# A hybrid SSD and forgetting-attention step on one core: values and dt columns by tokens, gate tiles spread over the stages

## The chip, the cores and the metric

The kernel runs on one core of one Trainium2 chip. The time is device microseconds of one execution; before the change the median of three runs is 2090.52 us (2086.51 to 2091.22). Lines named L242 and the like are lines of the kernel before.

## The reference, cut to what matters

One layer for 1024 new tokens of one stream and 16 tokens each of eight running streams, 1152 tokens in all, with a model width of 1024. One input projection yields the columns of two branches. The result, the new keys and values and the new states are returned.

```python
h = jnp.einsum('bld,de->ble', x, w_in)
z, xbc, dt_raw, q, k, v, f_raw, g_path, mg_m, mg_a = split_projection(h)
xbc, new_conv = causal_conv(xbc, conv_state, conv_w, conv_b)
dt = jax.nn.softplus(dt_raw + dt_bias)            # 32 heads
y, new_ssm = ssd_scan(xs, dt, A, Bm, Cm, s0, chunk)  # 8 groups
y_m = group_rms((y + d_skip * xs) * silu(z)) * mnorm_w
logf = jax.nn.log_sigmoid(f_raw + b_f)            # 16 heads
o = fox_prompt(q, k, v, logf)                     # and fox_sample, with caches
y_a = o * jax.nn.silu(g_path)
u = sigmoid(mg_m + b) * (y_m @ w_br_m) + sigmoid(mg_a + b) * (y_a @ w_br_a)
x_new = layer_norm(DN_ALPHA * x + u @ w_out, ln_g, ln_b)
```

## The kernel before, in words

Every f32 operand of a large product is split into a high and a low part of a reduced type, and a product becomes three: high by high, low by high, high by low. The input x stands in SBUF for the whole first half, as eight blocks of 128 rows (model width) by three chunks of 384 tokens, high and low. One **column tile** (`dense`, L257) is 128 output columns: for each of three chunks a PSUM bank gets 8 × 3 products (`passes`, L242 to L244, 128 by 128 stationary weights, 384 tokens moving) and is then taken out by a function that depends on the columns. So a column tile is 72 products, and its output has channels on partitions and tokens along the row. `fetch` and `split` (L202, L212) bring the next weight tile and split it, ScalarE the high part, another engine the low part.

The stages, in order:

1. **Head** (L311 to L339): x is loaded and split, and a column tile of only 48 columns (dt and forget columns) is computed, with channels on partitions; `tables` then transposes it to tokens (L357) and makes the decay tables from it.
2. **SSD stage**: eight groups of six column tiles (`group_dense`); beside the tiles of a group runs the scan of the group before (`group`). Behind the last group stand six of the 16 **gate tiles** (`gate_dense`, L717), whose output goes to DRAM.
3. **Attention stage** (FOX): eight pairs of heads. `pair_dense` computes four column tiles of a pair: values, gate path, queries, keys. The values must have tokens on partitions later, so 2 ticks after each of three banks three transposes (a **turn**, L745) and a copy bring them to `vt`. Beside the four tiles of a pair runs the attention of the pair before (`pair`), by a plan written out by hand: a list of ticks with what is issued at each. Beside the last pair run four gate tiles.
4. **Remaining gate tiles**: six, during which the SSD result is scaled. `ssr` loads sums of squares, takes root and reciprocal, writes `rs_d`; `load_rows` loads four blocks of rows (`yr`) and the scale (`rsb`), multiplies (L1151) and splits (L1154 ScalarE, L1155 VectorE) into `ya0`.
5. **Merge**: `quarter` and `whole` multiply the branch results by the branch weights into `acc`, apply the gates, then the output product (L1263 to L1265) and the layer norm.

What runs beside the tiles is a generator; `Flow` counts a tick for every two steps of eight in a bank, and lets the generator issue more when its ticks are used up. Inside `tc.manual_schedule()` instructions stay in the order written on each engine; outside, a scheduler orders them by priority. A pool of SBUF that reuses the room of a closed pool waits for that pool as a whole.

Of the kernel before, what the change touches and what calls it, by code (L numbers as in the profile page):

```python
# [11 lines left out]
F32 = mybir.dt.float32  # L12
# [22 lines left out]
GATES_SSD = 6  # L35
# [9 lines left out]
def in_tiles():  # L45
# [102 lines left out]
def trunk_step(ctx: ExitStack, tc: tile.TileContext, I, O):  # L148
# [35 lines left out]
    gate_d = dr.tile([16, P, T], F32, name="gate_d")  # L184

# [10 lines left out]
    todo = [(I["wdtf"], None, KT * 48)]  # L196
    todo += [(I["wt"][i], scale, 1024) for i, (_, scale) in enumerate(in_tiles())]
# [59 lines left out]
    def dense(rhs, evac, m=P):  # L257

        hi, lo = next_w()
        for c in range(NCH):  # L260
            d = bank(f"d{count[0]}_{c}")[:m, :CW]
            passes(d, KT, lambda k: (hi[:, k * m:(k + 1) * m], lo[:, k * m:(k + 1) * m]),
                   lambda k: (rhs[c][0][:, k, :], rhs[c][1][:, k, :]), lambda: evac(c, d))
# [23 lines left out]
    spa = ssd_stack.enter_context(tc.tile_pool(name="spa", bufs=1))  # L287


    pro_stack = ExitStack()  # L290
    pp = pro_stack.enter_context(tc.tile_pool(name="pp", bufs=1))
    dbf = pp.tile([48, 1], F32, name="dbf")
    sgn = pp.tile([48, 1], F32, name="sgn")
# [6 lines left out]
    dtf = pp.tile([48, T], F32, name="dtf")  # L300
# [4 lines left out]
    fones = pp.tile([P, P], F32, name="fones")  # L305

# [4 lines left out]
    fetch()  # L311
    split(more=False)
    ve.memset(sgn[0:32, :], 1.0)
    ve.memset(sgn[32:48, :], -1.0)
    for c in range(NCH):
        for h in range(4):
            k = slice(2 * h, 2 * h + 2)
            xr = pp.tile([P, 2, CW], F32, tag="xr", name=f"xr{c}_{h}", bufs=4)
            sy.dma_start(xr[:], I["xT"][c][:, k, :])
            ac.copy(X[c][0][:, k, :], xr[:])  # L320
            ve.tensor_tensor(X[c][1][:, k, :], xr[:], X[c][0][:, k, :].bitcast(F32), ALU.subtract)  # L321
        if c == 0:
            sy.dma_start(dbf[:], I["dtfb"])
    fetch()
    sy.dma_start(ident[:], I["ident"])
    sy.dma_start(cst[:], I["const"])
    sy.dma_start(cpro[:], I["const2"])
    sy.dma_start(alog[:], I["a_log"].to_broadcast([P, 32]))
    sy.dma_start(dsk[:], I["d_skip"].to_broadcast([P, 32]))
# [1048 lines left out]
```

## Time and profile before

| | |
|---|---|
| median of 3 runs | 2090.52 us |
| the profiled execution, its own time | 2090.63 us |
| its span | 2088.8 us |
| TensorE with work in flight | 2060.0 us, 14495 products |
| VectorE busy | 1331.9 us |
| ScalarE busy | 820.7 us |
| GpSimd busy | 615.8 us |
| granted TensorE clock, mean | 0.999 |
| mean DMA rate | 136 GB/s |

Times are in us from the span's start, unless marked ns. PE is TensorE, DVE VectorE, ACT ScalarE, POOL GpSimd, SP SyncE, whose queue issues most transfers. A row of a timeline has start, duration, engine, line, operation, output and inputs, shapes and a count; what follows in brackets is the time that the engine stood idle before it and what ended that. The durations of products overlap, since the array is pipelined; what a product costs is the distance from one start to the next.

### The profile page before, as it was taken

What the parts mean: (1) busy time and instruction counts of PE and PEld (TensorE: products, weight loads), DVE (VectorE), ACT (ScalarE), POOL (GpSimd) and SP (SyncE); (2) the same over time, 40 slices, a digit from 0 to 9 for tenths busy, and PEclk for the clock granted to TensorE, in tenths of its full rate; (3) what the DMA queues carried; (4) which work ended last, traced back from release to release, by engine and by line L of the source; (5) the groups of instructions that cost most, each with busy time, mean ns of one, the idle gap of its engine ahead of it and who ended that gap; (6) DMA issues with size and microseconds to landing.
All of it is one profiled execution on the core that took longest, in us unless ns stands there. A gap on an engine that the chain in (4) does not pass through costs nothing.

```text
span 2088.8 us, 36542 instructions
## 1 busy us (share of the span) xinstructions
PE 2060.0 (99%) x14495; PEld 1897.9 (91%) x14495; DVE 1331.9 (64%) x2252; ACT 820.7 (39%) x1662; POOL 615.8 (29%) x789
## 2 busy tenths in 40 slices
PE   8999999999999999999999999999999999999998
PEld 7998989898989898999889888889889999999987
DVE  7577777777777776514776866876765343182355
ACT  3344444444444343324455454454453442122210
POOL 1146465645555554510011011011111021113400
PEclk9999999999999999999999999999999999999999
DMA  5213242423232424443555555555564653154222
GB/s 169 81 55 106 88 121 81 133 76 127 76 117 77 126 76 133 133 153 100 199 177 190 189 193 170 190 193 176 182 204 148 219 195 108 41 188 154 86 100 91
DMA packets 110748, 283.07 MB, mean 136 GB/s; under 512 B 18041, under 2 KB 67185, under 8 KB 100337
## 3 DMA queue, kind: packets, MB, share of 16 engines
q1 hardware_dynamic: 98032, 199.46, 30.3%
q10 hardware_dynamic: 12544, 81.27, 11.2%
q8 instruction: 114, 1.87, 0.4%
q14 instruction: 58, 0.47, 0.1%
HBM read 228.89 MB, written 51.79 MB: 134 GB/s over the span
## 4 chain that ended last, share of the span: by engine, by line
PE 69%; DVE 18%; DMA 5%; ACT 4%; issue 2%; POOL 2%; SPq 0%; ACTq 0%; DVEq 0%; POOLq 0%
PE d L242 16%; PE d L244 15%; PE d L243 15%; PE o L903 3%; DVE m L605 3%; PE s L828 3%; DMA ce<-ac_d 2%; PE so L978 2%; PE out L1263 2%; PE out L1265 2%; PE out L1264 2%; PE dq L242 2%; PE dq L244 2%; PE dq L243 2%; DVE m L609 2%
## 5 line engine op out<-in xcount | busy, mean ns | idle before, releaser
L242 PE MATMUL d<-xh,wh 128*128 128x384 f32 (+1 forms) x2328 | 820.0, 352 | 16.9 <-ACT xh L320 6.2
L244 PE MATMUL d<-xh,wl 128*128 128x384 f32 (+1 forms) x2328 | 781.8, 336 | 0.1
L243 PE MATMUL d<-xl,wh 128*128 128x384 f32 (+1 forms) x2328 | 780.6, 335 | 0.8 <-DVE xl L321 0.7
L242 PEld LDWEIGHTS d<-xh,wh 128*128 128x128 f32 (+1 forms) x2328 | 436.1, 187 | 57.6 <-issue 18.1
L243 PEld LDWEIGHTS d<-xl,wh 128*128 128x128 f32 (+1 forms) x2328 | 436.7, 188 | 4.1 <-DVE xl L321 2.0
L244 PEld LDWEIGHTS d<-xh,wl 128*128 128x128 f32 (+1 forms) x2328 | 435.7, 187 | 1.7 <-DVE wl L225 0.4
L222 POOL TENSOR_TENSOR wl<-wr,wh 128x1024 fp32r<-128x1024 f32 (+1 forms) x58 | 137.6, 2372 | 319.5 <-ACT wh L221 304.6
L605 DVE TENSOR_SCALAR m<-ce,nacum 128x128 f32<-128x128 f32 x288 | 119.2, 455 | 49.5 <-DMA ce<-ac_d 49.4
L221 ACT CAST wh<-wr 128x1024 fp32r<-128x1024 f32 (+1 forms) x73 | 75.8, 1038 | 182.1 <-PE d L243 157.1
L833 ACT ACTIVATE st<-s,ckt 128x256 f32<-128x256 f32 (+1 forms) x320 | 115.0, 465 | 44.6 <-PE s L828 42.5
L225 DVE SCALAR_TENSOR_TENSOR wl<-wr,wh 128x1024 fp32r<-128x1024 f32 x50 | 61.7, 1235 | 60.1 <-ACT wh L224 60.1
L893 ACT ACTIVATE st<-st 128x1024 f32<-128x1024 f32 x80 | 82.0, 1065 | 44.1 <-DVE st L888 42.9
L837 POOL TENSOR_TENSOR st<-st,mask_bf 128x256 f32<-128x256 f32 x64 | 48.9, 784 | 161.9 <-ACT st L833 161.9
L778 POOL COPY knew<-kf 128x128 f32<-128x128 f32 x8 | 2.3, 290 | 241.5 <-ACT kf L775 241.5
L224 ACT ACTIVATE wh<-wr 128x1024 fp32r<-128x1024 f32 x50 | 52.8, 1056 | 51.8 <-PE d L243 42.9
L609 DVE TENSOR_TENSOR m<-m,cbm 128x384 f32<-128x384 f32 x96 | 70.7, 785 | 0.6
L607 ACT ACTIVATE ce<-ce 128x384 f32<-128x384 f32 (+1 forms) x96 | 46.8, 488 | 60.7 <-DVE m L605 60.7
L903 PE MATMUL o<-st,vt 128*64 128x256 f32 (+1 forms) x640 | 67.7, 362 | 0.0
L903 PEld LDWEIGHTS o<-st,vt 128*64 128x64 f32 x640 | 43.3, 137 | 24.6 <-issue 5.5
L243 PE MATMUL d<-yb0l,wh 128*128 128x384 f32 x192 | 64.1, 334 | 0.0
L243 PE MATMUL d<-yb1l,wh 128*128 128x384 f32 x192 | 64.1, 334 | 0.0
L242 PE MATMUL d<-yb0h,wh 128*128 128x384 f32 x192 | 64.1, 334 | 0.0
(621 smaller groups left out, 3922.8 us busy)
## 6 DMA issues: line engine op xcount, KB each, us to landing
wr<-in_wt SPq DMA_DIRECT2D x96, 512.0 KB
kc<-in_cache_k ACTq DMA_DIRECT2D x32, 1024.0 KB
vc<-in_cache_v ACTq DMA_DIRECT2D x32, 1024.0 KB
ce<-ac_d SPq DMA_DIRECT2D x96, 192.0 KB
wr<-in_wbr SPq DMA_DIRECT2D x24, 512.0 KB
gate_d<-gate SPq DMA_DIRECT2D x48, 192.0 KB
sb<-cs_d ACTq DMA_DIRECT2D x16, 576.0 KB
yr<-ym_d SPq DMA_DIRECT2D x16, 576.0 KB
```

Source lines behind the costliest of these rows:

```text
L221: ac.copy(hi[:, :cols], raw[:, :cols])
L222: lazy.get("sub", po).tensor_tensor(lo[:, :cols], raw[:, :cols], hi[:, :cols].bitcast(F32), ALU.subtract)
L225: ve.scalar_tensor_tensor(lo[:, :cols], raw[:, :cols], scale, hi[:, :cols].bitcast(F32), ALU.mult, ALU.subtract)
L242: te.matmul(out, wh, xh, start=(k == 0), stop=False)
L243: te.matmul(out, wh, xl, start=False, stop=False)
L244: te.matmul(out, wl, xh, start=False, stop=(k == n - 1))
L605: ve.tensor_scalar(m[:, j, :], ce[:, j * P:(j + 1) * P], nacum[:, b, h:h + 1], 0.0, ALU.add, ALU.min)
L609: ve.tensor_tensor(m[:], m[:], cbms[c][:], ALU.mult)
L828: te.matmul(ps2[:, e, 256 * x + q0:256 * x + 256], kk[hr, ks], qq[hr, qs], start=(at == 0), stop=(at == 2))
L833: ac.activation(S[j][:, e, kb, q0:], ps2[:, e, 256 * x + q0:256 * x + 256], AF.Identity, bias=ckt[:, kb, 2 * hp + e:2 * hp + e + 1])
L893: ac.activation(w, w, AF.Exp, scale=-1.0)
L903: te.matmul(o[64 * e:64 * e + 64, 256 * at + q0:256 * at + 256], vt[:, kb, 64 * e:64 * e + 64], S[j][:, e, kb, q0:256], start=(kb == 0), s ...
```

## The change

- The weights of the value columns are loaded whole (eight blocks of 128 by 1024, split in place), ahead of everything. For each block of 128 tokens and each half of 512 columns, x is now stationary and the weights move: `by_tokens`. The first three blocks are computed for both halves at once, in six banks, one step of 128 rows as its x block and its two weight halves arrive; the other six blocks follow. The values come out with tokens on partitions, go to the output (whose layout in DRAM changes) and to `v_d`, also in DRAM.
- The dt and forget columns follow in the same manner: 72 products of 96 columns (high and low weights side by side) and 72 of 48.
- `pair_dense` is cut into `gate_and_q` and `keys`. Value tiles and turns are gone; `keys` reloads the pair's values from `v_d` by one transfer on SyncE.
- The gate path and query tiles of the first pair now stand at the end of the SSD stage behind four gate tiles instead of six. Each of the next seven pairs has a gate tile where the value tile was; four still run beside the last pair; one is left ahead of the merge.
- Root and reciprocal of the scale (`rms`) are issued at the end of the second pair's plan. The row loads of the merge's first four blocks start beside the one last gate tile, all four at once (`early`), and end of the last pair's attention is issued by ticks there.
- Pools that reuse room wait for the single tiles that they overlap (`reuse_waits="tile"`), in place of whole pools.

```diff
-GATES_SSD = 6
+GATES_SSD = 4
...
     for hp in range(8):
-        order += [(V0 + 128 * hp, None), (G0 + 128 * hp, 0.5), (Q0 + 128 * hp, QSCALE), (K0 + 128 * hp, None)]
-    return order + gates[GATES_SSD:]
+        if hp:
+            order.append(gates[GATES_SSD + hp - 1])
+        order += [(G0 + 128 * hp, 0.5), (Q0 + 128 * hp, QSCALE), (K0 + 128 * hp, None)]
+    return order + gates[GATES_SSD + 7:]
...
+    def load_wv(k, n):
+
+        ns = slice(512 * n, 512 * n + 512)
+        raw = vp.tile([P, 512], F32, tag="wvr", name=f"wvr{k}_{n}", bufs=4)
+        sy.dma_start(raw[:], I["wv"][k][:, ns])
+        ac.copy(wv[k][0][:, ns], raw[:])
+        ve.tensor_tensor(wv[k][1][:, ns], raw[:], wv[k][0][:, ns].bitcast(F32), ALU.subtract)
+
+    def by_tokens(d, b, k, wh, wl):
+
+        c, js = b // 3, slice(b % 3 * P, b % 3 * P + P)
+        xh, xl = X[c][0][:, k, js], X[c][1][:, k, js]
+        te.matmul(d, xh, wh, start=(k == 0), stop=False)
+        te.matmul(d, xh, wl, start=False, stop=False)
+        te.matmul(d, xl, wh, start=False, stop=(k == KT - 1))
+
+    def value_product(d, b, n, k):
+        ns = slice(512 * n, 512 * n + 512)
+        by_tokens(d[:], b, k, wv[k][0][:, ns], wv[k][1][:, ns])
+
+    def value_out(d, b, n):
+        ns = slice(512 * n, 512 * n + 512)
+        vf = vp.tile([P, 512], F32, tag="vf", name=f"vf{b}_{n}", bufs=3)
+        ac.copy(vf[:], d[:])
+        sy.dma_start(O["v"][b][:, ns], vf[:])
+        sy.dma_start(v_d[b][:, ns], vf[:])
+
+    with tc.manual_schedule():
+        first = {(b, n): pt("tyu"[b], f"v{b}_{n}") for b in range(3) for n in range(2)}
+        for k in range(KT):
+            load_x(0, k, 1)
+            for n in range(2):
+                load_wv(k, n)
+            if k == 0:
+                fetch()
+            for n in range(2):
+                for b in range(3):
+                    value_product(first[b, n], b, n, k)
+        for c in range(1, NCH):
+            for k in range(0, KT, 2):
+                load_x(c, k, 2)
+        wd = vp.tile([P, 2, KT * 48], F32R, name="wd")
+        raw = vp.tile([P, 512], F32, tag="wvr", name="wdr", bufs=4)[:, :KT * 48]
+        sy.dma_start(raw, I["wdtf"])
+        ac.copy(wd[:, 0], raw)
+        ve.tensor_tensor(wd[:, 1], raw, wd[:, 0].bitcast(F32), ALU.subtract)
+        sy.dma_start(dbf[:], I["dtfb"].to_broadcast([P, 48]))
+        sy.dma_start(ident[:], I["ident"])
+        sy.dma_start(cst[:], I["const"])
+        sy.dma_start(cpro[:], I["const2"])
+        sy.dma_start(alog[:], I["a_log"].to_broadcast([P, 32]))
+        sy.dma_start(dsk[:], I["d_skip"].to_broadcast([P, 32]))
+        sy.dma_start(mcol[:], I["mnorm"])
+        sy.dma_start(bcol[:], I["b_merge"])
+        sy.dma_start(cw[:], I["conv_w"])
+        sy.dma_start(cb[:], I["conv_b"])
+        sy.dma_start(clf[:], I["cache_logf"])
+        split()
+        for b in range(3, 9):
+            for n in range(2):
+                d = pt("d", f"v{b}_{n}")
+                for k in range(KT):
+                    value_product(d, b, n, k)
+                value_out(d, b, n)
+                if b < 6:
+                    value_out(first[b - 3, n], b - 3, n)
+        u = pp.tile([P, 9, 48], F32, name="u")
+        for b0, n in ((0, 5), (5, 4)):
+            tp = pt("t", f"dtf{b0}")[:, :96 * n]
+            for b in range(b0, b0 + n):
+                c, js, at = b // 3, slice(b % 3 * P, b % 3 * P + P), 96 * (b - b0)
+                for k in range(KT):
+                    ks = slice(k * 48, k * 48 + 48)
+                    te.matmul(tp[:, at:at + 96], X[c][0][:, k, js], wd[:, :, ks], start=(k == 0), stop=False)
+                    te.matmul(tp[:, at:at + 48], X[c][1][:, k, js], wd[:, 0, ks], start=False, stop=(k == KT - 1))
+            tv = tp.rearrange("p (b i c) -> p b i c", i=2, c=48)
+            ub = u[:, b0:b0 + n, :]
+            ve.tensor_tensor(ub, tv[:, :, 0, :], dbf[:, None, :].to_broadcast([P, n, 48]), ALU.add)
+            ve.tensor_tensor(ub, ub, tv[:, :, 1, :], ALU.add)
+        ve.tensor_scalar(u[:, :, 32:48], u[:, :, 32:48], -1.0, None, ALU.mult)
+    v_stack.close()
+    spa = ssd_stack.enter_context(tc.tile_pool(name="spa", bufs=1, reuse_waits="tile"))
...
-        tp = pt("t", "dtft")
-        for b in range(9):
-            te.transpose(tp[:, b * 48:(b + 1) * 48], dtf[:, b * P:(b + 1) * P], ident[0:48, 0:48])
...
-        def evac_v(c, d):
-            vf = fp.tile([P, CW], F32, tag="kv1", name=f"vf{hp}_{c}", bufs=3)
-            ac.copy(vf[:], d)
-            sy.dma_start(O["v"][hp][:, ch(c)], vf[:])
-
-            def turn():
-                tp = pt("y", f"vt{hp}_{c}")
-                for j in range(3):
-                    te.transpose(tp[:, j * P:(j + 1) * P], vf[:, j * P:(j + 1) * P], ident[:])
-                ac.copy(vt[:, 3 * c:3 * c + 3, :], tp[:, :CW].rearrange("p (b d) -> p b d", b=3))
-
-            flow.after(2, turn)
-
-        dense(X, evac_v)
...
+    def keys(hp, r):
+        fp = lazy["fp"]
+        vt = r["vt"] = fp.tile([P, 9, P], F32, tag="vt", name=f"vt{hp}", bufs=2)
+        sy.dma_start(vt[:], v_d[:, :, P * hp:P * hp + P].rearrange("b p d -> p b d"))
...
+        if hp == 1:
+            plan.insert(-1, (82.0, 0.0, (lazy["rms"],)))
...
+    r = gate_and_q(0)
...
+        r = keys(0, r)
         for hp in range(1, 8):
             flow.start(pair(hp - 1, r))
-            r = pair_dense(hp)
+            gate_dense(GATES_SSD + hp - 1, fp, "kv1", 3)
+            r = keys(hp, gate_and_q(hp))
         flow.start(pair(7, r))
-        for j in range(GATES_SSD, GATES_SSD + GATES_FOX):
+        for j in range(GATES_SSD + 7, GATES_SSD + 7 + GATES_FOX):
...
+    def load_rows(src_y, kts, slots, norm, first_pool=mp, early=1, delay=0, pace=3):
+
+
+        rb, ys, kts = {}, {}, list(kts)
+
+        def send(kt):
+            ys[kt] = mp.tile([P, T], F32, tag="yr", name=f"yr{norm}{kt}", bufs=4)
+            sy.dma_start(ys[kt][:], src_y[kt])
+            g = kt // 2
+            if norm and g not in rb:
+                pool = mp if rb else first_pool
+                rb[g] = pool.tile([P, T], F32, tag="rsb", name=f"rsb{kt}", bufs=1)
+                sy.dma_start(rb[g][:], rs_d[g:g + 1, :].to_broadcast([P, T]))
+
+        for kt in kts[:early]:
+            send(kt)
+        yield delay
...
     A0 = a_slots("ya0")
-    flow.start(load_rows(ym_d, range(0, 4), A0, 1))
-    for j in range(GATES_SSD + GATES_FOX, 16):
-        gate_dense(j, mp, "gt", 4)
-    flow.drain()
+    with tc.manual_schedule():
+        flow.start(load_rows(ym_d, range(0, 4), A0, 1, ap, 4, 5, 2))
+        flow.step()
+        after = lazy.pop("after")
+        flow.after(2, after[0])
+        flow.after(4, after[1])
+        for j in range(GATES_SSD + 7 + GATES_FOX, 16):
+            gate_dense(j, mp, "gt", 4)
+        flow.drain()
+    for fn in after[2:]:
+        fn()```

Where it moves instructions, on TensorE at the start of the program: before, the 48-column tile (`d3`, from weight tile 0), with transposes of its result (`dtft`) between the first group's products (`d4`):

```order
L242 MATMUL d3_0_204<-xh0_89,wh0_131 48x384
L243 MATMUL d3_0_204<-xl0_90,wh0_131 48x384
L244 MATMUL d3_0_204<-xh0_89,wl0_132 48x384
...
L242 MATMUL d4_0_291<-xh0_89,wh1_198 128x384
L357 MATMUL dtft_315<-ident_79,dtf_123 128x48 x3
L243 MATMUL d4_0_291<-xl0_90,wh1_198 128x384
```

and now, where `v0_0` is the first half of token block 0, `v1_0` that of block 1, and `dtf0` the dt columns of the first five blocks:

```order
L332 MATMUL v0_0_146<-vh0_128,xh0_90 128x512
L333 MATMUL v0_0_146<-vl0_129,xh0_90 128x512
L334 MATMUL v0_0_146<-vh0_128,xl0_91 128x512
L332 MATMUL v1_0_148<-vh0_128,xh0_90 128x512
...
L334 MATMUL v8_1_791<-vh7_142,xl2_95 128x512
L393 MATMUL dtf0_821<-wd_426,xh0_90 128x96
L394 MATMUL dtf0_821<-wd_426,xl0_91 128x48
```

The narrow tile and its transposes have gone from the first place, and 432 value products and 144 short ones stand ahead of the first group.

On TensorE in the attention stage, in the second chunk of the first of four tiles beside the first pair: before, the value tile of the second pair (`d62`) with a turn in it:

```order
L242 MATMUL d62_1_10236<-xh1_91,wh59_10030 128x384
L243 MATMUL d62_1_10236<-xl1_92,wh59_10030 128x384
L244 MATMUL d62_1_10236<-xh1_91,wl59_10031 128x384
L745 MATMUL vt1_0_10243<-ident_79,vf1_0_10195 128x128 x3
L242 MATMUL d62_1_10236<-xh1_91,wh59_10030 128x384
```

and now a gate tile (`d58`) there:

```order
L244 MATMUL d58_1_10640<-xh1_92,wh55_10435 128x384
L245 MATMUL d58_1_10640<-xl1_93,wh55_10435 128x384
L246 MATMUL d58_1_10640<-xh1_92,wl55_10436 128x384
L244 MATMUL d58_1_10640<-xh1_92,wh55_10435 128x384
L245 MATMUL d58_1_10640<-xl1_93,wh55_10435 128x384
```

The wide products are as many as before, and the three transposes are gone.

On VectorE between the last pair's attention and the merge (`rows7` is the last pair's reciprocal sums, `yr10` to `yr13` the four blocks of rows, `ya0` their split form, `wl` low parts of weights): before

```order
L1002 RECIPROCAL rows7_17341<-rows7_17341 64x32
L225 SCALAR_TENSOR_TENSOR wl92_17378<-wr92_17164,wh92_17377 128x1024
L225 SCALAR_TENSOR_TENSOR wl93_17508<-wr93_17381,wh93_17507 128x1024
L1137 RECIPROCAL ssr_17366<-ssr_17366 128x72
L1151 SCALAR_TENSOR_TENSOR yr10_17390<-yr10_17390,mcol_83,rsb0_17392 128x1152
```

and now

```order
L1052 RECIPROCAL rows7_17719<-rows7_17719 64x32
L1216 SCALAR_TENSOR_TENSOR yr10_17667<-yr10_17667,mcol_84,rsb0_17669 128x1152
L1220 TENSOR_TENSOR ya0l0_17660<-yr10_17667,ya0h0_17659 128x384
L1220 TENSOR_TENSOR ya0l1_17662<-yr10_17667,ya0h1_17661 128x384
L1220 TENSOR_TENSOR ya0l2_17664<-yr10_17667,ya0h2_17663 128x384
L1216 SCALAR_TENSOR_TENSOR yr11_17671<-yr11_17671,mcol_84,rsb0_17669 128x1152
```

The weights of five gate tiles and the scale's reciprocal no longer stand between the last pair and the rows of the merge.

More of the change, by code (lines that the diff above doesn't have):

```diff
@@ L305, in trunk_step @@
     fones = pp.tile([P, P], F32, name="fones")
+    v_stack = ExitStack()
+    vp = v_stack.enter_context(tc.tile_pool(name="vp", bufs=1))
+    wv = [(vp.tile([P, D], F32R, name=f"vh{k}"), vp.tile([P, D], F32R, name=f"vl{k}")) for k in range(KT)]
     def CP(n):
@@ L309, in CP @@
         return cpro[:, at:at + w]
[L311 to L323, printed above, removed]
```

159 lines of the change are left out of this document (75 added, 84 removed).

## The prediction, before the change was run

> **What bounds the kernel now.** I read the page's busy times first, then the waits of TensorE, then the windows.
>
> ```profile
> span 2088.8 us, 36542 instructions
> PE 2060.0 (99%) x14495; PEld 1897.9 (91%) x14495; DVE 1331.9 (64%) x2252; ACT 820.7 (39%) x1662; POOL 615.8 (29%) x789
> ```
>
> TensorE has work in flight in 2060.0 of 2088.8 us, and the next engine, VectorE, in 64%. So the answer must be sought on TensorE: what it executes, and the 28.8 us without a product. The waits of TensorE alone (waiter, what it waited for, us, times, longest) say how little of that is spread out:
>
> ```profile
> PE d L242 <- ACT xh L320: 6.2, 2, 5.9
> PE acmc L862 <- DVE ext L857: 2.5, 3, 1.8
> PE d L242 <- ACT raw0c L463: 1.7, 1, 1.7
> PE vt L745 <- ACT vf L739: 0.4, 1, 0.4
> ```
>
> 5.9 us is the start, before the first data; the longest other one is 1.8 us. A busy TensorE need not be at its rate, so I read how many products a window holds (us, then busy and count of PE):
>
> ```profile
> 1700.00:1800.00 100.00, 100.00 (x579) 100.00 (x578) 33.91 (x48) 25.52 (x48) 19.39 (x8) 1.00 0.34 112
> 0.00:26.33 26.33, 19.05 (x95) 12.28 (x95) 14.85 (x24) 13.21 (x17) 1.78 (x10) 1.00 0.82 269
> ```
>
> In the merge, pure 384-wide products run at 100/579 = 0.173 us each. The first 26.33 us hold 95 products, where 152 would fit: the head is the one stretch that is badly filled. Everything else is worth only the products that go away.
>
> **The change part by part.** All sums are against the profiled execution's own 2090.63 us (span 2088.80 and 1.83 around it), which is the median of the runs, 2090.52, to 0.1 us.
>
> *Values by tokens instead of by columns.* Eight column tiles of 3 × 8 × 3 = 72 products of width 384 go: 576 × 0.173 = 99.7 us. Nine row blocks × 2 halves × 8 × 3 = 432 products of width 512 come. The output product is of that shape (start, duration):
>
> ```profile
> 2029.81 0.39 PE L1263 MATMUL out<-wh,uh 128*128 128x512 f32 x1
> 2030.04 0.40 PE L1264 MATMUL out<-wl,uh 128*128 128x512 f32 x1
> ...
> 2031.19 0.40 PE L1263 MATMUL out<-woh,uh 128*128 128x512 f32 x1
> ```
>
> Six starts in 1.38 us are 0.230 us each, so 432 × 0.230 = 99.4 us: **-0.3**.
>
> *The turns go.* Each pair turned its values with three groups of three transposes. One such place on TensorE, in order of start, and the group of all:
>
> ```profile
> 975.26 0.34 PE L244 MATMUL d<-xh,wl 128*128 128x384 f32 x1
> 975.43 0.49 PE L745 MATMUL vt<-ident,vf 128*128 128x128 f32 x3
> 975.68 0.42 PE L242 MATMUL d<-xh,wh 128*128 128x384 f32 x1
> 975.94 0.33 PE L243 MATMUL d<-xl,wh 128*128 128x384 f32 x1
> ...
> L745 PE MATMUL vt<-ident,vf 128*128 128x128 f32 x72 | 11.8, 272 | 0.4 <-ACT vf L739 0.4
> ```
>
> From 975.26 to 975.94 there are 0.68 us for two wide products that need 0.35, so a group of three costs 0.33 us, of which TensorE's full queue hides nothing. 72/3 = 24 groups: **-8.0**, and the wait of 0.4 us with them: **-0.4**. Two copies on ScalarE with each group go too; TensorE waited for them only those 0.4 us, so they count zero. In their place the SyncE queue issues one reload of 576 KB per pair, in 512-byte pieces, ahead of the fourth of four column tiles. What stands behind it in that queue is the next weight tile, a whole tile ahead of its use; TensorE's first use of the reloaded values comes with the next pair's first `values` step (tick 35.8 of its plan), over 35 us later. Zero, if the extra traffic leaves the bias rows alone (a rival, below).
>
> *The head.* These are TensorE's first products, ScalarE's first casts, which show when a transfer had landed, and SyncE's first issues:
>
> ```profile
> 5.89 0.56 PE L242 MATMUL d<-xh,wh 128*48 128x384 f32 x1 [5.89 <-ACT xh L320]
> ...
> 7.24 0.53 PE L244 MATMUL d<-xh,wl 128*48 128x384 f32 x1
> 7.55 0.53 PE L242 MATMUL d<-xh,wh 128*48 128x384 f32 x1
> ...
> 10.44 0.41 PE L242 MATMUL d<-xh,wh 128*48 128x384 f32 x1
> 19.14 0.57 PE L357 MATMUL dtft<-ident,dtf 48*128 48x48 f32 x6
> 3.22 0.51 ACT L221 CAST wh<-wr 128x384 fp32r<-128x384 f32 x1 [1.20 <-DMA wr<-in_wdtf]
> 5.01 1.79 ACT L320 CAST xh<-xr 128x768 fp32r<-128x768 f32 x2 [1.28 <-DMA xr<-in_xT]
> 0.74 0.39 SPq L209 DMA_DIRECT2D wr<-in_wdtf  x1
> L917 DVE TENSOR_TENSOR fs<-st 128x512 f32<-128x512 f32 x32 | 22.1, 690 | 0.8
> L357 PE MATMUL dtft<-ident,dtf 48*128 48x48 f32 x9 | 1.0, 230 | 0.0
> ```
>
> Before: of the 95 products 72 are the dt tile and 9 its transposes, so 14 × 0.173 = 2.4 us of the 26.33 are work that stays, and the head costs 23.9 us. After: the first transfer is again 192 KB and lands at about 3.2; the 256 KB behind it by about 4.1 (the next one, of twice 192 KB, was cast from 5.01 on); a cast of some 0.5 and a subtraction of 0.69 later, at 5.1, the products run without a hole. The first ones start 0.31 to 0.32 us apart, until 10.44: for 4.6 us TensorE does half its work, and that loses 2.1 us again. (The Trainium skill, TensorE: Matmul & The Clock Gate, The HAM clock gate, says that the array passes half its pulses until it has been busy for some 3.4 us; by that the loss is 1.6 us. The trace agrees with the half rate and shows a longer stretch.) Then the supply: 708 KB for each of eight steps, against 18 × 0.230 = 4.1 us of products. At the 269 GB/s of the window 0 to 26.33 that is 2.6 us, so transfers stay ahead, and VectorE's three subtractions of at most 0.69 us fit as well. The 18 copies out and their 36 stores lie beside products: a block and half is 24 × 0.230 = 5.5 us, there are two banks to alternate, and a copy takes about 0.5; without that cover they would cost 18 × 0.5 = 9 us.
>
> The dt columns come as 72 products of width 96 and 72 of width 48, each with a stationary block of its own. No row has this shape. Lower end, by the dt transposes: six of width 48 take 0.57 us, less the last's 0.22 that is 0.07 us each, so 144 × 0.07 = 10.1 us. Upper end: a product in full f32 is two records, as the state products are (8 groups × 8 blocks in the code, 128 in the trace):
>
> ```profile
> L577 PE MATMUL dS<-wx,bt 128*128 128x256 f32 x128 | 31.5, 378 | 0.0
> ```
>
> A record of width 128 in a turn cost 0.33/3 = 0.11, so 72 × (0.22 + 0.14) = 25.9. I take one record each, the wide ones between 0.07 and 0.11: 72 × (0.09 + 0.07) = 11.5, because these operands are of the reduced type whose products of width 384 are one record. Head after: 5.1 + 2.1 + 11.5 = 18.7, so **-5.2** (from -6.6 to +9.2).
>
> *SSD stage.* The order on every engine is unchanged in it, and so are its small waits: 0. That the waits between pools are now for single tiles counts zero too: the rows above show no wait of TensorE of over 1.8 us after the start, so there is nothing for them to free; they are what lets the next part be late only a little.
>
> *The gate tiles.* All 16 stay, so TensorE's work is the same. But of six that stood between attention and merge, one is left. Before, TensorE's last products of attention, VectorE's end of it, and then the row loads:
>
> ```profile
> 1605.75 0.34 PE L244 MATMUL d<-xh,wl 128*128 128x384 f32 x1
> 1605.91 0.35 DVE L985 TENSOR_SCALAR os<-so,ssum 128x128 f32<-128x128 f32 x1
> 1621.34 0.43 SPq L1145 DMA_DIRECT2D yr<-ym_d  x1
> 1628.02 0.32 SPq L1150 DMA_DIRECT2D rsb<-rs_d  x1
> 1634.15 1.42 DVE L1151 SCALAR_TENSOR_TENSOR yr<-yr,mcol,rsb 128x1152 f32<-128x1152 f32 x1 [9.28 <-DMA rsb<-rs_d]
> 1635.61 1.34 ACT L1154 CAST ya0h<-yr 128x384 fp32r<-128x384 f32 x3 [2.09 <-DVE yr L1151]
> 1638.03 1.41 DVE L1151 SCALAR_TENSOR_TENSOR yr<-yr,mcol,rsb 128x1152 f32<-128x1152 f32 x1
> 1650.86 1.96 DVE L1155 TENSOR_TENSOR ya0l<-yr,ya0h 128x384 fp32r<-128x384 f32 x4
> ```
>
> Rows of the scale took 6.1 us from issue (1628.02) to use (1634.15). In the new order SyncE issues the row loads right behind the last store of the gate tile that ends at 1605.75, about 1.5 us later; nothing but row work is queued behind them on VectorE. So VectorE starts some 8 us after 1605.75 and needs 1.42 and three subtractions of 0.5 behind a cast of 0.5, 3.4 us, for each of four rows: the fourth row's first third is ready 8 + 3 × 3.4 + 2.5 = 20.7 us after 1605.75. TensorE has one gate tile, 72 × 0.173 = 12.5, and the 54 products over the first three rows that its order puts ahead, 9.4, together 21.9. It holds by 1 us; the transfers are six at once, and a cast of the next weights (1.04) stands among ScalarE's. I take **+1.5** (0 to 8).
>
> *The scale's square root* moves into the second pair, on ScalarE, ahead of a key tile's last copy:
>
> ```profile
> 1622.54 1.28 ACT L1136 ACT_TABLE_LOAD   x1
> ```
>
> Two such loads and 0.4 us of work, 3 us once, with a wait for a small transfer. Behind them wait the copy and eight score evacuations; two banks of scores and one of products cover it. **+0.5** (0 to 3).
>
> Sum: -0.3 - 8.0 - 0.4 - 5.2 + 1.5 + 0.5 = -11.9, so **2078.7 us**.
>
> **The rivals.** 0.2% is 4.2 us, about what a measurement of this kernel tells from no change.
>
> *Merge starved (slower).* The chain ahead of the merge is long and has lost 62 us of cover. Before, it ran from 1605.75 to 1652.8, 47 us. If the new tiles still wait for attention's, or the six transfers and VectorE come as they did then, TensorE waits 47 - 22 = 25 us, less the 1.5 counted: 2078.7 + 23.5 = 2102. It is slower once the chain passes 22 + 1.5 + 11.9 + 4.2 = 40 us. Against it: 16 us of the 47 were pool handover before 1621.34 and 7 the scale, which is now made a stage earlier. (The Trainium skill, TensorE: Matmul & The Clock Gate, The HAM clock gate, has the array fall back to half rate after an idle window of some 3.4 us, which would add about 2 us; no wait in this trace after the start is long enough to show it.) Chance 0.07.
>
> *Dear dt columns (no change).* If the narrow products go at the full f32 price, the head gains nothing: 2078.7 + 14.4 = 2093. Chance 0.09. (The Trainium skill, TensorE: Matmul & The Clock Gate, Wait — 56ns, not 53.3ns?, gives some 62 ns as the sequencer's bound for a short product; 144 × 0.062 = 8.9 us would be 2.6 less than I take. The 0.07 of the transposes agrees.)
>
> *Late bias rows in attention (smaller gain).* One wait of TensorE followed a bias load that took 7.65 us:
>
> ```profile
> 1541.38 7.65 DMA sb<-cs_d
> 1554.28 0.30 PE L862 MATMUL acmc<-ident,ext 128*128 128x128 f32 x1 [1.79 <-DVE ext L857]
> ```
>
> The reloads add eight transfers of that size. If each pair then loses 0.8 us: 2078.7 + 6.4 = 2085. Against it: they are issued half a pair away from the first bias load. Chance 0.14, two thirds of it still faster by over 0.2%.
>
> **How the numbers follow.** That the change doesn't do what it says needs no chance: the turns are gone from TensorE's order. The forecast has the remaining 0.70. Its own lower end is 2073 (dt at its lower end -1.4, merge and square root free -2.0, attention's three waits of 2.5 gone), its upper end 2085 (the merge at 8 instead of 1.5). Faster: 0.68 + 0.09 = 0.77; no change: 0.02 + 0.05 + 0.08 = 0.15; slower: 0.08, the starved merge and a little of the dear columns. The range reaches from 2071, 1.7 us lower for the one larger wait of the SSD stage that a shifted start could close, to 2087, through the late bias rows.
>
> **What would show it.** Right: TensorE's products start near 5 us and fill 10 to 100 us without holes, the group of turns is gone, 144 narrow products take 10 to 12 us, the SSD and attention stages keep their length but for 1 us per pair, and TensorE waits under 3 us where the merge's first products read ya0. Wrong: a wait of 10 us or more there, narrow products 0.15 us apart, or attention pairs as long as before.

## The result and the profile after

The changed kernel takes 2105.12 us, the median of four runs (2100.61 to 2106.25), against 2089.69 us for the kernel before in the same runs (2086.51 to 2091.22): a ratio of 1.0072 (1.0052 to 1.0091). It is slower; the prediction of 2078.7 us, its range and its sign were wrong. The profiled execution took 2104.45 us. From here on, lines named L242 and the like are those of the kernel whose view is shown.

The page after: span, TensorE's busy time, and the clock that TensorE was granted, in 40 slices of 52.6 us:

```profile
span 2102.6 us, 36247 instructions
PE 2065.9 (98%) x14342; PEld 1892.9 (90%) x14342; DVE 1341.0 (64%) x2265; ACT 811.6 (39%) x1644; POOL 616.0 (29%) x787
PEclk9979999999999999999999999999999999999999
```

TensorE holds 153 recorded products fewer than before (14495) and is yet busy 5.9 us longer. The third slice says why to look at 105 to 158 us: the granted clock is 0.7 there. Windows cut at the first narrow product, at the two places where the clock changes, and at the first dense tile (PE busy and count, and the clock in the column behind POOL):

```profile
4.66:108.24 103.58, 103.58 (x433) 82.81 (x433) 24.58 (x38) 31.36 (x52) 2.50 (x2) 1.00 0.57 193
108.24:112.62 4.38, 4.38 (x41) 4.38 (x40) 0.00 (x0) 0.59 (x1) 0.00 (x0) 1.00 0.48 145
112.62:134.79 22.17, 22.17 (x107) 22.17 (x106) 0.81 (x2) 0.00 (x0) 0.00 (x0) 0.50 0.00 0
134.79:139.73 4.94, 4.94 (x16) 4.94 (x17) 3.78 (x6) 1.13 (x2) 0.00 (x0) 0.50 0.02 3
```

The narrow products of the dt columns run from 108.24 to 134.79, 26.55 us, and TensorE has work in flight in every bit of it. After 4.38 us the clock falls to 0.50 and stays there until 4.94 us of 384-wide products have run. TensorE's timeline where it falls and where it comes back:

```profile
112.40 0.29 PE L393 MATMUL dtf<-wd,xh 128*128 128x96 f32 x1
112.53 0.25 PE L394 MATMUL dtf<-wd,xl 128*128 128x48 f32 x1
112.62 0.41 PE L393 MATMUL dtf<-wd,xh 128*128 128x96 f32 x1
112.83 0.37 PE L394 MATMUL dtf<-wd,xl 128*128 128x48 f32 x1
113.03 0.43 PE L393 MATMUL dtf<-wd,xh 128*128 128x96 f32 x1
...
139.41 0.52 PE L246 MATMUL d<-xh,wl 128*128 128x384 f32 x1
139.73 0.45 PE L244 MATMUL d<-xh,wh 128*128 128x384 f32 x1
140.02 0.34 PE L245 MATMUL d<-xl,wh 128*128 128x384 f32 x1
140.19 0.34 PE L246 MATMUL d<-xh,wl 128*128 128x384 f32 x1
```

Two narrow products take 0.22 us from start to start at full clock (112.40 to 112.62) and 0.41 to 0.43 at half clock (from 112.62 on); a dense one 0.32 instead of 0.17.

TensorE's waits after, to be read against those of before in the prediction:

```profile
PE acmc L912 <- DVE ext L907: 11.9, 7, 3.0
PE v L332 <- ACT vh L325: 4.7, 1, 4.7
PE dq L245 <- DVE ya0l L1220: 2.7, 2, 2.0
```

The start is 1.2 us earlier than before (4.7 for 5.9). The merge waits 2.7 us, as foreseen in kind (`dq`). But `acmc`, the transpose of a pair's c unit (the minima of its third set of scores, brought across partitions), waited 2.5 us in three pairs before and waits 11.9 us in seven now. One such pair, from the transpose of the sums of the pair before (`acs`), on several engines:

```profile
1361.45 0.27 PE L912 MATMUL acs<-ident,ext 128*128 128x128 f32 x1
1362.68 0.48 SPq L1053 DMA_DIRECT2D rc_d<-rows  x1
1364.42 1.25 SPq L1058 DMA_DIRECT2D rb<-rc_d  x2
1369.35 2.40 POOL L1061 TENSOR_TENSOR gs<-gs,rb 128x1024 f32<-128x1024 f32 x1 [2.68 <-DMA rb<-rc_d]
1371.78 0.60 ACTq L990 DMA_DIRECT2D sb<-cs_d  x1
1379.33 1.23 DVE L1011 CUSTOM_DVE_ANT_0 ps<-ss,sb 128x1024 f32<-128x1024 f32 x1 [2.83 <-DMA sb<-cs_d]
1384.44 0.30 PE L912 MATMUL acmc<-ident,ext 128*128 128x128 f32 x1 [1.26 <-DVE ext L907]
```

and the same places of a pair in the kernel before:

```profile
1369.17 0.27 PE L862 MATMUL acs<-ident,ext 128*128 128x128 f32 x1
1377.62 2.40 POOL L1011 TENSOR_TENSOR gs<-gs,rb 128x1024 f32<-128x1024 f32 x1 [3.25 <-DMA rb<-rc_d]
1380.05 0.60 ACTq L940 DMA_DIRECT2D sb<-cs_d  x1
1387.17 1.22 DVE L961 CUSTOM_DVE_ANT_0 ps<-ss,sb 128x1024 f32<-128x1024 f32 x1 [2.30 <-DMA sb<-cs_d]
1392.29 0.30 PE L862 MATMUL acmc<-ident,ext 128*128 128x128 f32 x1 [0.36 <-DVE ext L857]
```

It is one chain in both. The sums make a round trip through DRAM, GpSimd multiplies by them (`rb`), and only then may the bias rows be asked for, because they share `rb`'s buffer: `sb` is issued 0.03 us behind the end of GpSimd's 2.40. They land some 7.5 us later, VectorE adds them, and folds the minima that TensorE transposes. The chain takes 23.1 us before (1369.17 to 1392.29) and 23.0 after (1361.45 to 1384.44). What changed is TensorE: without its wait it comes to `acmc` after 22.8 us before (23.12 - 0.36) and after 21.7 now (22.99 - 1.26). The 1.0 us between is one pair's three turns. They stood in the place of a wait.

One of the two long ones among these waits (2.96 and 3.03 us) costs more than its own length. Its product, and a window from there on (third column from the end: the clock):

```profile
1222.07 0.45 PE L912 MATMUL acmc<-ident,ext 128*128 128x128 f32 x1 [2.96 <-DVE ext L907]
1222.00:1225.40 3.40, 3.33 (x11) 3.36 (x12) 2.55 (x4) 0.55 (x1) 0.00 (x0) 0.50 0.55 184
```

For 3.4 us behind the wait of 2.96 us the granted clock is 0.50. From `acmc` to the next transposes (`tps`) twelve dense products then take 3.74 us, where they take 2.22 in the pair shown above (1384.44 to 1386.66): 1.5 us more. The wait of 3.03 us before 1629.75 is not followed by such a spell, so a wait of this size brings it only in some cases.

### The profile page after: what moved, and what is told of

Read it like the earlier page. It is cut to its first block, busy times and chain, and to the rows that moved or that the text cites. A ratio compares the mean times of both kernels' runs of the same rounds, so it can differ in the third digit from the quotient of the medians.

```text
span 2102.6 us, 36247 instructions
## 1 busy us (share of the span) xinstructions
PE 2065.9 (98%) x14342; PEld 1892.9 (90%) x14342; DVE 1341.0 (64%) x2265; ACT 811.6 (39%) x1644; POOL 616.0 (29%) x787
## 4 chain that ended last, share of the span: by engine, by line
PE 72%; DVE 14%; DMA 7%; ACT 3%; issue 2%; POOL 2%; SPq 0%; DVEq 0%; ACTq 0%; POOLq 0%
PE d L244 15%; PE d L245 14%; PE d L246 14%; PE o L953 3%; DVE m L664 2%; DMA ce<-ac_d 2%; DMA sb<-cs_d 2%; PE s L878 2%; PE v L332 2%; PE v L333 2%; PE v L334 2%; PE so L1028 2%; PE out L1343 2%; PE out L1341 2%; PE out L1342 2%
## 5 line engine op out<-in xcount | busy, mean ns | idle before, releaser
L244 PE MATMUL d<-xh,wh 128*128 128x384 f32 x2112 | 746.5, 353 | 8.7 <-ACT raw7c L522 1.0
L246 PE MATMUL d<-xh,wl 128*128 128x384 f32 x2112 | 709.7, 336 | 0.0
L245 PE MATMUL d<-xl,wh 128*128 128x384 f32 x2112 | 708.9, 336 | 0.0
L244 PEld LDWEIGHTS d<-xh,wh 128*128 128x128 f32 x2112 | 398.2, 189 | 46.0 <-issue 18.1
L245 PEld LDWEIGHTS d<-xl,wh 128*128 128x128 f32 x2112 | 398.7, 189 | 0.8
L246 PEld LDWEIGHTS d<-xh,wl 128*128 128x128 f32 x2112 | 397.6, 188 | 0.0
L224 POOL TENSOR_TENSOR wl<-wr,wh 128x1024 fp32r<-128x1024 f32 x56 | 133.8, 2389 | 360.1 <-ACT wh L223 360.1
L223 ACT CAST wh<-wr 128x1024 fp32r<-128x1024 f32 x64 | 66.9, 1045 | 193.9 <-PE d L245 156.5
L943 ACT ACTIVATE st<-st 128x1024 f32<-128x1024 f32 x80 | 81.5, 1064 | 47.5 <-DVE st L938 46.7
L953 PE MATMUL o<-st,vt 128*64 128x256 f32 (+1 forms) x640 | 68.0, 362 | 1.2 <-ACT st L943 1.1
L953 PEld LDWEIGHTS o<-st,vt 128*64 128x64 f32 x640 | 43.3, 137 | 26.2 <-issue 5.7
L244 PE MATMUL d<-yb0h,wh 128*128 128x384 f32 x192 | 64.1, 334 | 0.0
L245 PE MATMUL d<-yb0l,wh 128*128 128x384 f32 x192 | 64.1, 334 | 0.0
L246 PE MATMUL d<-yb0h,wl 128*128 128x384 f32 x192 | 64.1, 334 | 0.0
L244 PE MATMUL d<-yb1h,wh 128*128 128x384 f32 x192 | 64.1, 334 | 0.0
L245 PE MATMUL d<-yb1l,wh 128*128 128x384 f32 x192 | 64.1, 334 | 0.0
```

The lines of the kernel that those rows point to most:

```text
L223: ac.copy(hi[:, :cols], raw[:, :cols])
L224: lazy.get("sub", po).tensor_tensor(lo[:, :cols], raw[:, :cols], hi[:, :cols].bitcast(F32), ALU.subtract)
L244: te.matmul(out, wh, xh, start=(k == 0), stop=False)
L245: te.matmul(out, wh, xl, start=False, stop=False)
L246: te.matmul(out, wl, xh, start=False, stop=(k == n - 1))
L943: ac.activation(w, w, AF.Exp, scale=-1.0)
```

## The experiments

Theories: **A**, few columns per time halve the clock, without a gap in TensorE's work; against it **B**, narrow products or stationary blocks are dear by themselves. **C**, the turns covered the chain of the bias rows; against it the rival on record, that the reloads of the values delay them, and any other thing that is late there. Times are beside runs of the kernel before on the same chip, whose medians were 2090.5, 2090.1 and 2091.7 us in the three sets.

**Wide dt products.** All 144 are 384 wide; the kernel leaves out the selection of the dt columns, so its dt means nothing:

```diff
-te.matmul(tp[:, at:at + 96], X[c][0][:, k, js], wd[:, :, ks], start=(k == 0), stop=False)
-te.matmul(tp[:, at:at + 48], X[c][1][:, k, js], wd[:, 0, ks], start=False, stop=(k == KT - 1))
+te.matmul(tw[:, ws], X[c][0][:, k, js], wd[:, 0, :], start=(k == 0), stop=False)
+te.matmul(tw[:, ws], X[c][1][:, k, js], wd[:, 1, :], start=False, stop=(k == KT - 1))
```

> Against the changed kernel (2105.1 us), whose 144 narrow products of the dt columns (96 and 48 wide) take 26.55 us, 4.4 us of them at full clock (0.223 us for two) and the rest at half clock (0.427 us for two). Here the same 144 products, with the same stationary blocks, are each 384 wide; the values of dt are wrong and the time alone is read. Theory A (the clock is halved when few columns pass per time, although products follow each other without a gap): no half clock after 15 us, 144 x 0.174 = 25.1 us, the first dense tile behind it at 0.174 instead of 0.320, so 2101 us in all, no slower than with narrow products. Theory B (each product with a stationary block of its own, or the stretch itself after 430 wide products, halves the clock): the clock falls here too, 144 products then take about 0.32 each, 42 us, and the kernel 2120 us.

One run: 2098.7 us. The window of these products:

```profile
108.73:134.17 25.44, 25.44 (x146) 25.44 (x145) 0.81 (x2) 0.59 (x1) 0.00 (x0) 1.00 0.08 25
```

Over five times the columns (768 instead of 144 per two products) in 1.1 us less, at clock 1.00. For the clock A holds and B falls: neither the number of products nor their stationary blocks halve the clock.

**128 and 192 wide.** The same edit with slices of 128 and of 192 columns.

> As the wide trial, but the 144 products of the dt columns are 128 wide (values of dt wrong, time alone is read). At full clock a product with a stationary block of its own takes about 0.11 us, as a turn does, so 128 columns per 0.11 us pass, half of what passes at 384 wide and nearly twice the 144 columns per 0.223 us of the changed kernel. If the clock is halved below some share between, it falls here too after 4 to 5 us and the 144 products take 30 us; if not, they take 16 us at full clock, 2092 us in all. I hold it open, and expect the half clock rather than not, 0.5 to 0.5.

> The same at 192 wide, about 192 columns per 0.11 us. Theory A expects no half clock here (0.7 of what passes beside products 384 wide): 144 x 0.11 = 16 us, 2092 us in all. With the half clock it would be 144 x 0.2 = 29 us, 2107 us.

2090.52 and 2095.52 us, one run each. The window of the 128-wide ones:

```profile
107.89:123.92 16.03, 16.03 (x146) 16.03 (x144) 0.81 (x2) 0.58 (x1) 0.00 (x0) 1.00 0.14 40
```

No half clock in this window, nor in that of the 192-wide ones (108.59 to 124.65), so the half clock, held open and rather expected at 128, did not come. The 5.0 us between the two runs lie elsewhere: the run with 192 has four later spells of 3.41 us at clock 0.50, the other two, each behind a wait of 2.0 to 3.3 us. Starts are 0.112 us apart at 128 and at 192 alike: 16.0 and 16.1 us for the 144. Two of 96 and 48 took 0.22. So at full clock such products cost 0.11 us each on average at widths from 48 to 192, and the bound of the clock lies between 144 columns in 0.223 us (0.65 per ns, halved) and 128 in 0.112 us (1.14 per ns, not halved). Where in between was not tried.

**Narrow products spread.** Each two are issued behind three 512-wide ones:

```diff
                 for k in range(KT):
                     value_product(d, b, n, k)
+                    if (b, n) >= (4, 1):
+                        dt_product(*narrow.pop(0))
```

> The two narrow products of each block and row of x are issued behind three 512-wide value products each, from the 24th such group on, instead of all at the end. Theory A (half clock by few columns per time): no half clock after the start; each two cost at most the 0.223 us that they took at full clock, 72 x 0.223 = 16.1 us, and the 2.7 us of slow dense products behind them go: 2105.1 - 10.5 - 2.7 = 2092 us or less; about 2083 if the loads of stationary blocks hide behind wide products and two narrow ones cost 0.1 us. Theory B (a narrow product costs 0.18 us whatever stands beside it): 2105 less the 2.7 us of the dense tile at most, 2102 us.

2089.27 us, ratio to the kernel before 0.9994 (0.9984 to 1.0004): 16 us won, and no half clock in this stretch (its trace has three spells of 3.41 us at clock 0.50 later on, behind waits of 2.9, 2.0 and 2.0 us). Its timeline on TensorE:

```profile
73.20 0.40 PE L334 MATMUL v<-vh,xl 128*128 128x512 f32 x1
73.44 0.21 PE L388 MATMUL dtf<-wd,xh 128*128 128x96 f32 x1
73.48 0.25 PE L389 MATMUL dtf<-wd,xl 128*128 128x48 f32 x1
73.58 0.48 PE L332 MATMUL v<-vh,xh 128*128 128x512 f32 x1
73.89 0.39 PE L333 MATMUL v<-vl,xh 128*128 128x512 f32 x1
```

From 73.44 to 73.89 are 0.45 us for two narrow products and one wide one that takes 0.23: the narrow ones still cost 0.22 together. Wide neighbours keep the clock up, but do not hide their price.

**Turns back as mere work.** Behind each of the seven gate tiles beside pairs three groups of three transposes whose output nobody reads:

```diff
+            def turn():
+                tp = pt("y", f"vt{j}_{c}")
+                for i in range(3):
+                    te.transpose(tp[:, i * P:(i + 1) * P], t[:, i * P:(i + 1) * P], ident[:])
+
+            if tag == "kv1" and j < GATES_SSD + 7:
+                flow.after(2, turn)
```

> Each of the seven gate tiles beside a pair is followed by three groups of three 128-wide transposes whose results nobody reads, where the values were turned in the kernel before; 21 groups, by the trace of before 0.33 us each, 6.9 us of work added. Theory C (the removed turns only covered a wait): the waits before the transposes of the c units fall by 0.5 to 1 us per pair, and the time stays within 3 us of 2105. Rival (the turns were worth their time, and the waits have a cause of their own): the waits stay at 13 us, 2105 + 7 = 2112 us.

2107.86 us (ratio to before 1.0079, 1.0064 to 1.0094): 2.7 more than the changed kernel for 6.9 us of work; the intervals of the two overlap, so the time alone does not settle it. The waits at `acmc` say more: 8.7 us in six pairs, for 11.9 in seven. In the three pairs with turns whose chain is of the usual length they are 0.0 to 0.4 us, where the changed kernel has 0.8 to 1.6 in such pairs, as C says; but the sum did not go back to 2.5, so C does not explain all of it. In three pairs of this run GpSimd's product started 9.4 to 9.9 us after the transpose of the sums, in the other four 7.9 to 8.3, and those three make most of the waits, 2.1 to 2.6 us each.

**Reloads for two pairs only.** The six other pairs use the first two pairs' values; six reloads are left out, and the output means nothing.

```diff
+        if hp < 2:
+            vts[hp] = fp.tile([P, 9, P], F32, tag="vt", name=f"vt{hp}", bufs=2)
+            sy.dma_start(vts[hp][:], v_d[:, :, P * hp:P * hp + P].rearrange("b p d -> p b d"))
+        vt = r["vt"] = vts[hp % 2]
```

> The changed kernel with the values reloaded for the first two pairs only; the other six use those, so their output is wrong and the traffic of six reloads is left out. Theory C2 (a chain that the reloads have no part in): waits at the c units of 10 to 13 us as in the changed kernel, 2102 to 2106 us. The rival on record (the reloads delay the bias rows, 0.8 us per pair): the waits fall to about 5 us, 2097 to 2099 us.

One run, 2104.03 us, and its wait at the c units:

```profile
PE acmc L916 <- DVE ext L911: 13.2, 7, 3.2
```

With six of eight reloads left out the wait is as long as before, so the reloads have no part in it. The rival on record had the right place and nearly the right size (6.4 us, against 9.4), and the wrong cause.

**Bias rows asked for at 5.4 instead of 15.4.** `rb` goes to the idle buffer of the probabilities:

```diff
-            rb = S["rb"] = fq.tile([P, 4, 256], F32, tag="sbias", name=f"rb{hp}", bufs=1)
+            rb = fp.tile([P, T], F32, tag="prob", name=f"rb{hp}", bufs=1)[:, :SEQ].rearrange("p (j q) -> p j q", q=256)
...
-            (5.4, 0.0, (least, 3, 1)),
+            (5.4, 0.0, (s_bias, 0), (least, 3, 1)),
```

> The bias rows of a pair's first half get a buffer of their own (the rows of the pair before, which shared it, go to the idle buffer of the probabilities) and are asked for at 5.4 of the plan instead of 15.4. Theory C (in the changed kernel TensorE waits 13.0 us before the transposes of the pairs' c units because the bias rows, whose load waits for GpSimd's last product of the pair before and then takes 7.7 us, come too late; in the kernel before, where a group of turns lay in this place, it waited 3.5 us): these waits fall below 1 us in all, 2105.1 - 12 = 2093 us. Rival (what comes late at these places is something else, such as VectorE's own work or TensorE's scores): at most 3 us less, 2102 us or more.

2106.33 us (ratio to before 1.0072, 1.0057 to 1.0087): nothing won, the waits are 13.4 us. Neither theory, as written. Its chain in one pair:

```profile
1363.04 0.60 ACTq L990 DMA_DIRECT2D sb<-cs_d  x1
1364.06 0.48 SPq L1053 DMA_DIRECT2D rc_d<-rows  x1
1370.86 1.25 SPq L1062 DMA_DIRECT2D rb<-rc_d  x2
1375.74 2.38 POOL L1065 TENSOR_TENSOR gs<-gs,rb 128x1024 f32<-128x1024 f32 x1 [7.70 <-issue]
```

The 576 KB of bias rows are now issued 1.0 us ahead of a store of 8 KB, and the reload behind that store waits 6.8 us (1364.06 to 1370.86) where it waited 1.7 (1362.68 to 1364.42 above). The sums are late in place of the bias rows. So the chain holds two transfers, the sums and the bias rows, and the large one must stand clear of the small round trip.

**Bias rows asked for a pair earlier**, at 62.6 of its plan (`rb` as above, none at 15.4 but in the first pair):

```diff
-            (62.6, 0.0, (load, "v", hp, 1, 1)),
+            (62.6, 0.0, (load, "v", hp, 1, 1), (s_bias, 0, 1)),
```

> As the early bias rows, but the load is asked for in the pair before, at 62.6 of its plan, so that it neither waits for GpSimd's product nor runs beside the small store and loads of the row sums, which the earlier trial delayed (from the store of the sums to the loads behind it 6.9 us instead of 1.8). Theory C2 (TensorE waits at the c units because a chain of 22.5 to 24.8 us runs from the transpose of the sums: store and reload of the sums, GpSimd's product, the bias rows behind it, VectorE's work; its own work up to there is 21.4 us): with the bias rows out of the chain VectorE's step on them starts about 16.5 us after that transpose instead of 17.4 to 19.6, and the seven waits fall from 13.0 to below 2 us: 2105.1 - 11 = 2094 us. Rival (another thing is late in this place): waits of 8 us or more, 2101 us or more.

2101.79 us (ratio to before 1.0057, 1.0042 to 1.0073). The waits at `acmc` are gone, 0.2 us from the start of one product to the next in all seven, which settles that this chain made them. But only 3.3 us are won. The first line of this kernel's waits:

```profile
PE o L953 <- ACT st L943: 10.3, 13, 1.4
```

and its small round trip of the a unit's minima:

```profile
1411.84 0.60 ACTq L994 DMA_DIRECT2D sb<-cs_d  x1
1412.69 0.32 SPq L926 DMA_DIRECT2D mn_d<-rowma  x1
1419.69 0.32 SPq L929 DMA_DIRECT2D mb_a<-mn_d  x1
1423.66 3.50 DVE L938 TENSOR_TENSOR st<-st,mb_a 128x1024 f32<-128x1024 f32 x3 [2.40 <-DMA mb_a<-mn_d]
```

against the changed kernel's:

```profile
1415.16 0.32 SPq L926 DMA_DIRECT2D mn_d<-rowma  x1
1419.00 0.32 SPq L929 DMA_DIRECT2D mb_a<-mn_d  x1
```

Behind the large load the round trip takes 7.0 us from issue to issue, without it 3.8; in the first seven pairs it is 5.3 to 7.0 here, and 3.7 to 3.9 in six of the changed kernel's, 6.1 in the seventh. One wait was taken away, and a new one made in its place.

**The same with spread products, and in the kernel before.** No further edit.

> The changed kernel with its two losses mended: narrow products spread (which alone gave 2089.3) and bias rows asked for a pair earlier. If the two are independent, 2089.3 - 11 = 2078 us, faster than the kernel before (2090.5) by 12 us, which is about the gain that the turns and the head promised. Rival (the waits come back in another place, since VectorE or the scores are next): 2085 us or more.

> The kernel before with bias rows asked for a pair earlier. Theory C2: its seven waits before the transposes of the c units, 5.0 us in all (0.3 to 0.7 in six pairs, 2.1 in the last), fall below 1.5 us: 2090.5 - 3 to 4 = 2087 us. So the same edit that is worth 11 us in the changed kernel is worth a third of that here, since the turns stood in this place. Rival (the edit itself saves time elsewhere): 2082 us or less.

2089.84 us (0.9998, 0.9989 to 1.0007) and 2098.18 us (1.0036, 1.0022 to 1.0050). In the first the rival came out: the waits moved to the values products, 13.9 us. In the second neither theory did: the values products wait 6.6 us there. The edit harms the kernel before, in which there was little to win.

**Bias rows asked for at 71.8 of the pair before**, when that round trip is over:

```diff
-            (71.8, 0.0, (weights, 0, 0, 1)),
+            (71.8, 0.0, (weights, 0, 0, 1), (s_bias, 0, 1)),
```

> Spread narrow products, and the bias rows asked for in the pair before, at 71.8 of its plan instead of 62.6. In the trial at 62.6 the seven waits at the c units fell to 0.18 us each, but 576 KB asked for just ahead of the small store of the a unit's minima made its way out and back 5.0 to 7.0 us instead of 3.8, and TensorE then waited 10 to 14 us before the values products. Theory C3 (the two places are the only tight ones; a large load is harmless where no small round trip is under way): both waits are gone, 2089.3 - 9 to 11 = 2079 us. Rival (every place is tight, and the large load or the loads that it pushes back make a third wait): 2086 us or more.

> The same shift of the bias rows, to 71.8, in the kernel before. At 62.6 it made that kernel slower by 8 us, through the small round trip. Theory C3: its waits at the c units, 5.0 us, fall to 1.3 us and nothing takes their place: 2090.1 - 3.5 = 2086.6 us. Rival (a third wait): 2092 us or more.

With spread products: **2080.8 us**, ratio to the kernel before 0.9944 (0.9931 to 0.9958), faster than both. The longest of its waits, none of them at `acmc` or at the values products:

```profile
PE v L332 <- ACT vh L325: 4.5, 1, 4.5
PE s L886 <- ACT st L891: 3.6, 2, 3.1
PE dq L245 <- DVE ya0l L1236: 2.5, 2, 2.0
```

3.6 us are new, in the one pair behind the scale's square root, and the clock is at 0.50 for 6.8 us behind them. The trace shows where they come from:

```profile
1167.39 0.60 ACTq L1002 DMA_DIRECT2D sb<-cs_d  x1
1169.64 0.53 SPq L1168 DMA_DIRECT2D ssr<-ss_d  x1
1182.17 0.35 ACT L1169 ACTIVATE ssr<-ssr,epst 128x72 f32<-128x72 f32 x1 [8.72 <-DMA ssr<-ss_d]
```

The bias rows are now issued 2.2 us ahead of the small load for the root, which is used 12.5 us after its issue (1169.64 to 1182.17), where it was 4.85 in the changed kernel (1184.68 to 1189.53). ScalarE waits 8.7 us for it, and the score evacuations behind it, for which TensorE waits, come late. So the rival of a third wait came out in one pair; that the large load makes it is read from the two traces, and no run tested it. In the kernel before the same shift gives 2089.44 us (0.9988, 0.9978 to 0.9997), 2.3 us instead of the 3.5 expected. So the two mends are worth 24 us in the changed kernel (27 by the ratios to the kernel before), and freed of what it set loose the change is worth some 9 us (2089.4 to 2080.8), where 11.9 were predicted.

## Why the prediction was wrong, step by step

The gap is 2104.45 - 2078.7 = 25.75 us.

- **The dt columns, +15.1, and the tile behind them, +2.3.** The step that failed: "I take one record each, the wide ones between 0.07 and 0.11: 72 × (0.09 + 0.07) = 11.5". Each is one record, as supposed. But two cost 0.223 us at full clock, 16.1 in all; the row of six transposes 48 wide, from which 0.07 came, was no measure for products with a stationary block of 128 by 128 each (theirs were 48 by 128). The other 10.5 us are the half clock, and it goes on into 15 dense products that take 4.94 us instead of 2.6. The upper end of 25.9 was near 26.55 by accident: no full f32 price is in it. The prediction reckoned with a slow clock only at the start and after a wait, and the one after a wait came too: the 1.5 us below. (The Trainium skill, TensorE: Matmul & The Clock Gate, What's actually happening, has the clock set by how busy the array has lately been, and gives an idle window as what brings the half rate back; here it came back at 112.62, behind 108 us without idle time, so few columns had that effect too.)
- **The turns, +9.4, and the clock behind a wait, +1.5.** The step that failed: "a group of three costs 0.33 us, of which TensorE's full queue hides nothing". The price was right and the cover overlooked: the turns stood on the near side of a chain that TensorE was already about to wait for. Before's own trace showed it: the only pair without turns beside it, the last, was the one with the 1.79 us that the prediction quoted for a late bias load. 1.0 us per pair in six pairs makes 6.2 of the 9.4; the rest is largely the chain itself, 1.3 to 1.6 us later in two pairs. One of them has the scale's square root ahead of it, and the wait of 2.96 us with its spell of half clock behind it; no run took that apart. The lengths agree: from the first pair's scores to the merge's first product it took 720.1 us before (961.41 to 1681.51) and 661.7 after (1032.36 to 1694.06); five gate tiles (62.4) and 21 turns (6.9) should have made it 650.8, which is 10.9 less.
- **Values, +2.1.** 103.58 us instead of 99.4 + 2.1 for the slow start: their starts are 0.234 apart instead of 0.230 in the output product. The start itself came 0.4 us earlier than taken.
- **The merge, -0.3.** TensorE waits 2.7 us in it, but from its first product to the end it takes 408.5 us for 407.3, 1.2 more where 1.5 was counted; the rival of a starved merge, 25 us of wait, stayed away.
- **SSD stage, -3.7.** "0" was too cautious. Up to the first product of the first pair's scores it took 937.5 us before (from 26.33 to 961.41, with 2.4 us of it ahead) and 895.3 after (from 134.79 to 1032.36, less the 2.3 of half clock); three column tiles of 12.5 and one pair's turns make 38.5 of the 42.2 us between. Why the rest was won was not tested.

With the earlier start (-0.4) these add up to +26.0. The 0.5 counted for the square root comes off, since what it cost is within the turns' line: 25.5 of the 25.75 us. The reloads cost nothing, as predicted. (The 708 KB of a supply step in the prediction are 192 + 2 × 256 = 704; nothing hangs on it.) The chance of 0.08 for slower was too small for a reason that can be named: each of the two unknowns had a rival, but both rivals were priced as one mechanism apiece, and none asked what a saved microsecond would run into next.

## What to carry to other kernels

A TensorE that the profile calls busy without a gap can still lose half its clock: look at the granted clock of each stretch, and do not put narrow products in a row; spread them among wide ones or widen them. Before counting a removed instruction as time won, follow the next thing that TensorE waits for back to its start and compare the lengths of both ways; a pair or tile that already lacks the instruction shows the answer. A large load does harm when it is issued just ahead of a small store whose reload somebody waits for, so move it to where no such round trip is under way. Every small transfer that somebody waits for counts there: at 71.8 the load seems to have met another one.

## What was not expected of the hardware

- 144 columns per 0.223 us, without a gap, brought the granted clock from 1.00 to 0.50 after 4.38 us; 128 per 0.112 us did not.
- A product with a stationary block of its own took 0.112 us at full clock for 128 and for 192 columns, and two of 96 and 48 took 0.22, between wide products too.
- A wait of TensorE of 2.96 us was followed by 3.4 us at granted clock 0.50, which cost 1.5 us more; one of 3.03 us in the same run was not.
- An 8 KB store just behind a load of 576 KB on another queue held up its reload for 6.8 us instead of 1.7.
